# Riding head gates in recurrent weight tiles, compression steps of two chunks, and attention sums in pairs

## The chip, the cores and the metric

One core of a Trainium2 chip. The metric is the device time of one execution in microseconds (us); lower is better. Besides TensorE (PE in the profile, its weight loads PEld) a core has VectorE (DVE), ScalarE (ACT), GpSimd (POOL) and SyncE (SP), whose queue issues the weight transfers here.

## What is computed

Two layers of a first block (mixer of three branches, cross attention, convolutional MLP) and one layer of a second block, on 256 tokens of width 1024, all in float32. The parts that the change touches:

```python
# first block, in each of two layers
out_a = window_attention(aq, ak, av, a_sink)       # 8 heads of 64, 2 key heads
out_b = dense_block_attention(bq, bk, bv)          # the same shape, no mask
...
# second block
(u_rnn, u_gate, q, k_c, v_c, k_s, v_s, k_w, v_w, g_nsa, g_a, g_b) = jnp.split(xn @ w_in, cuts, axis=-1)
h_a = rg_lru(causal_depthwise_conv(u_rnn, conv_w, conv_b), ...)   # u_rnn: 1344 = 12 * 112 columns
...
kc = rmsnorm(compress_blocks(kv(k_c), phi_k_pe, phi_k_w1, phi_k_w2), kc_norm)
vc = compress_blocks(kv(v_c), phi_v_pe, phi_v_w1, phi_v_w2)
gates = jax.nn.sigmoid(g_nsa...)                   # 16 heads x 3 = 48 columns
...
def compress_blocks(z, pe, w1, w2):                # 15 blocks of 32 tokens, 4 groups
    ...
    return jax.nn.gelu(flat @ w1, approximate=True) @ w2
```

## The kernel before

All weights stream through the chip once. `Stream` (L174) brings them in chunks of 128 x 1024 (512 KB): SyncE starts the transfer into `raw` (4 buffers), ScalarE casts it to `wh` (L220), VectorE takes the rest `wl` = `raw` - `wh` (L221), and the product with the activations, themselves split into a high and a low part, is three float32r matmuls for each weight tile (`mm_a`, L402 to L404, or `mm_b`, L416 to L418). A chunk of eight 128-wide tiles is 24 matmuls over the 256 tokens. `take` (L224) gives out a chunk; the next two are split ahead of it.

TensorE's order is written by hand: the order of the calls is its order. Each `take` is followed by a tick (L341), which first gives out what `later(n, f)` has put off by n ticks and then one step of each background generator. So the attention runs between the chunks of other products: `attend` (L721) issues the scores of a unit (two heads, one token tile), `probs_t` (L713) some ticks later, which transposes the probabilities into `pt`, and `sums` some ticks after that. The order of ScalarE and VectorE is made by the tile scheduler, from what the program issues and what waits for what.

`gqa` (L734) makes the units of an attention of block 1. Its `sums` multiply the values with `pt` for two heads at a time: eight matmul records in the trace (four instructions, L757), each with 64 of the array's columns, into one PSUM tile `tp`, which `split` (L386) then takes out: ScalarE the high half `oh` (L388), VectorE the low half `ol` (L389). `tp` (L337) has two buffers; the transposes of `probs_t` use the same name. In each layer there are two attentions of four such sums. `head_norm` (L786) runs beside the first of them; its factor comes from GpSimd (`rstd`, L371), and its second half is L809, the rotation L773, L778 and L784 on VectorE.

In the second block the chunk `gn` holds the 48 columns of the head gates, padded to 128. Its product gives `gs`, which `gates` transposes two ticks later (L1527). Then come the recurrent branch (`lru_steps`, L1244, chunks `ur`, `ug`, `lga`, `lgx`; tiles 112 wide) and, between its first eight chunks, `phi_steps` (L1167), the first layer of the compression MLPs: a `pkv` chunk a step, used in float32 straight from `raw`, eight records with 60 columns each (L1177). `lru_tail` (L1295) and the selected attention `nsa_units` (L1324) run in the background.

```python
ATT = (2,) * 8 + (1, 2) * 4, 4, 2
def tp(self, shape=(128, 4, 128)):
    return self.ps.tile(list(shape), F32, name="tp", bufs=2)
```

Of the kernel before, what the change touches and what calls it, by code (L numbers as in the profile page):

```python
# [19 lines left out]
S = 256  # L20
# [19 lines left out]
TURN = 2  # L40
WARM = 7
# [6 lines left out]
def pack_a(w, nw=128, kw=128, per=8):  # L48
    """[K, N] -> one chunk of `per` stationary tiles after the other, N outer and K inner."""
    k, n = w.shape  # L50
    t = w.reshape(k // kw, kw, n // nw, nw).transpose(2, 0, 1, 3).reshape(-1, kw, nw)
    c = t.shape[0] // per
    return np.ascontiguousarray(t.reshape(c, per, kw, nw).transpose(0, 2, 1, 3).reshape(c, kw, per * nw))


def pack_b(w):
    """[K, N] -> chunks of two 128-row tiles of 512 columns, N outer and K inner."""
    k, n = w.shape
    t = w.reshape(k // 128, 128, n // 512, 512).transpose(2, 0, 1, 3).reshape(-1, 2, 128, 512)
    return np.ascontiguousarray(t.transpose(0, 2, 1, 3).reshape(-1, 128, 1024))  # L60


def feat(v, w=128):
    """[..., N] -> [w, ..., N // w]: features on partitions."""
# [11 lines left out]
def layout(x):  # L76
    """The arrays the program reads: the inputs cut and ordered, and constants of the shapes."""
# [55 lines left out]
def layout2(f, o):  # L133
# [4 lines left out]
    o["ur"], o["ug"] = pack_a(ur, RW), pack_a(ug, RW)  # L138
# [4 lines left out]
    o["gn"] = pack_a(np.pad(gn.reshape(D, 16, 3)[:, :, [1, 2, 0]].transpose(0, 2, 1).reshape(D, 48), ((0, 0), (0, 80))))  # L143
# [30 lines left out]
class Stream:  # L174
    """The weights in the order of their use: each chunk comes in ahead of its products and is split
    into two float32r parts whose sum is the float32 weight."""
# [10 lines left out]
    def load(self, i, piece=None):  # L187
# [7 lines left out]
        else:  # L195
            # the very first chunk, in two pieces of 512 columns
# [46 lines left out]
    def take_last(self, key, places, more):  # L243
        """The last chunks of a product, as many as places and two, and those behind them, all on chip at once;
        those behind the first two have their room in places, the third one behind and on in more."""
# [5 lines left out]
    def hold(self, after):  # L251
        """The next chunks are split after the instructions `after`."""
        self.after, self.until = after, self.split + 2


class Program:
    def __init__(self, ctx, tc, a, out):
# [41 lines left out]
        # products that raise the tensor engine's clock while the first loads are on their way  # L299
# [4 lines left out]
    def order2(self, add):  # L304
        add("q2", len(EARLY))
        for key in ("k2", "v2", "cc", "gn"):
            add(key)
        n = 0
        for kind, b in LRU_ORDER:
            for i in range(2 if kind == "b" else 3):  # L310
                if kind == "b":
                    add("lgx" if i else "lga", b, b + 1)
                else:
                    add("ur" if kind == "u" else "ug", 3 * b + i, 3 * b + i + 1)
                if n < 8:
                    add("pkv", n, n + 1)
                n += 1
        for key in ("ga", "pa", "gb", "pb", "wo2", "minb", "min", "mout"):
            add(key)

    # ---- small helpers
# [18 lines left out]
    # ---- the order of the tensor engine: a tick before the products of each chunk  # L340
    def tick(self):  # L341
        """Gives out what is due, then a step of everything in the background."""
# [14 lines left out]
    def spawn(self, g):  # L357
        """Runs the first step of g now, the others a tick apart."""
# [3 lines left out]
    def wait(self):  # L362
        """What follows on the vector engine comes after the split of the last chunk."""
        return self.tc.issue_after(self.w.last.ins)

    def settle(self):
        """Gives out all that is left in the background."""
# [3 lines left out]
    def rstd(self, pool, var, eps, n, scale=1.0):  # L371
        """(var * scale + eps) ** -0.5 in float32, Newton's method from the exponent halved."""
# [13 lines left out]
    def split(self, h, l, src):  # L386
        """float32r parts h + l of src (SBUF or PSUM)."""
# [7 lines left out]
    def mm_a(self, ps, w, xs, nw=128, kw=128, t0=0, start=True, stop=True):  # L395
        """ps [nw, S] += W^T x: stationary tiles t0.. of the chunk w against the feature-major xs."""
# [9 lines left out]
    def mm_b(self, outs, ws, xs, kt, ts=(0, 1)):  # L406
        """outs[t] [128, 512] += x W for chunk list ws covering k-tiles kt.. of kt_n."""
# [12 lines left out]
    def mm_b_first(self, outs, wt, xs):  # L420
        """mm_b with the very first chunk, in the order in which the parts come."""
# [8 lines left out]
    def proj_b(self, key, xs, kn=8):  # L430
        """Token-major product with a [K, 512] weight."""
# [41 lines left out]
    def turn(self, outs, n, done):  # L473
        """Feature-major tiles [128, 2, S] of a token-major product: done(i, tile) n ticks later."""
# [15 lines left out]
    def take_early(self, key):  # L490
        """Takes the chunks that come before the next one of `key`."""
# [29 lines left out]
    def q(self, op, *args, **kw):  # L521
        """An instruction of the vector engine in the order of these calls."""
# [21 lines left out]
    def to_fm(self, t, halves, dst):  # L544
        """Token tile t, by halves, to its feature-major high parts in dst, then the low parts."""
# [77 lines left out]
        # sums by halves, squares about the mean of the first half: var = E[(x - m0)^2] - (m - m0)^2  # L623
# [59 lines left out]
    def softmax(self, s, scale, sink=None, mask=None):  # L683
        """Scores s (PSUM [128, 2, 256]) of two heads -> normalised probabilities [128, 2, 256]."""
# [28 lines left out]
    def probs_t(self, pr, pt, t):  # L713
        """Probabilities of token tile t transposed into pt [keys, head, key tile, tokens]."""
# [926 lines left out]
```

## Time and profile before

| | |
|---|---|
| time, median of 3 runs | 1471.21 us (1470.07 to 1471.54) |
| profiled execution, its span | 1467.7 us |
| TensorE busy | 1446.2 us, 99% of the span |
| VectorE, ScalarE busy | 1083.6 us, 889.3 us |
| HBM read | 254.89 MB, 174 GB/s |

The runs lie 2.4 to 3.8 us above the span of the profiled execution, which is what the trace covers. A timeline row reads: start in us, duration in us, engine, line, operation, output tile <- input tiles, shape, count, and in brackets the idle time before it and what ended it. The timeline draws consecutive instructions of one kind together, and a matmul's duration is a modelled one that overlaps the next; from start to start is what the engine spends.

### The profile page before, as it was taken

How to read it: one execution, taken by the hardware profiler on the slowest of the kernel's cores; microseconds unless marked ns; L12 is line 12 of the kernel's file. 1: busy time of each engine (PE TensorE's matmuls, PEld its weight loads, DVE VectorE, ACT ScalarE, POOL GpSimd, SP SyncE). 2: the span in 40 equal slices, each digit the busy share in tenths (PEclk: the TensorE clock that was granted, in tenths of full speed). 3: DMA queues.
4: the chain of work that ended last, by engine and by line, in shares of the span. 5: the costliest groups of instructions: out<-in, count | busy, mean ns of one | idle time of the engine just before them, and what ended most of it. 6: DMA issues, size and time to landing. Idle time of an engine off the chain costs nothing.

```text
span 1467.7 us, 26006 instructions
## 1 busy us (share of the span) xinstructions
PE 1446.2 (99%) x9919; PEld 1315.4 (90%) x9919; DVE 1083.6 (74%) x2195; ACT 889.3 (61%) x1608; POOL 46.0 (3%) x134
## 2 busy tenths in 40 slices
PE   9999999999999999999999999999999999999998
PEld 7889988899988899998889998788989999899887
DVE  6887576788857888668688885886889785866543
ACT  5866555666645586555666665464888775555432
POOL 1110000000000020000000000120100000000000
PEclk9999999999999999999999999999999999999999
DMA  8554574555566544454736566356544445555563
GB/s 314 172 159 158 177 225 127 187 188 186 179 186 216 186 145 147 141 197 164 253 105 205 184 199 221 129 171 190 172 121 141 134 149 168 191 164 183 185 202 99
DMA packets 75192, 257.63 MB, mean 176 GB/s; under 512 B 9787, under 2 KB 11196, under 8 KB 74940
## 3 DMA queue, kind: packets, MB, share of 16 engines
q1 hardware_dynamic: 75067, 255.97, 54.5%
q8 instruction: 78, 1.28, 0.3%
q14 instruction: 47, 0.38, 0.1%
HBM read 254.89 MB, written 1.05 MB: 174 GB/s over the span
## 4 chain that ended last, share of the span: by engine, by line
PE 82%; DVE 7%; ACT 5%; DMA 3%; issue 2%; POOL 1%; SPq 0%; DVEq 0%; ACTq 0%; POOLq 0%
PE mm L402 15%; PE mm L403 15%; PE mm L404 15%; PE mm L417 8%; PE mm L418 8%; PE mm L416 8%; DVE wl L221 2%; PE mm L455 2%; PE mm L457 2%; PE mm L458 1%; ACT wh L220 1%; PE tp L718 1%; PE tp L757 1%; PE tp L552 1%; PE sc L680 1%
## 5 line engine op out<-in xcount | busy, mean ns | idle before, releaser
L221 DVE TENSOR_TENSOR wl<-raw,wh 128x1024 fp32r<-128x1024 f32 (+3 forms) x434 | 521.0, 1206 | 236.8 <-ACT wh L220 230.7
L220 ACT CAST wh<-raw 128x1024 fp32r<-128x1024 f32 (+3 forms) x434 | 447.1, 1036 | 403.9 <-PE mm L403 141.3
L402 PE MATMUL mm<-fmh,wh 128*128 128x256 f32 (+1 forms) x1736 | 493.8, 284 | 3.8 <-ACT gates L957 1.7
L403 PE MATMUL mm<-fml,wh 128*128 128x256 f32 (+1 forms) x1736 | 490.6, 283 | 0.0
L404 PE MATMUL mm<-fmh,wl 128*128 128x256 f32 (+1 forms) x1736 | 490.6, 283 | 0.0
L402 PEld LDWEIGHTS mm<-fmh,wh 128*128 128x128 f32 (+1 forms) x1736 | 329.1, 190 | 9.1 <-issue 2.9
L403 PEld LDWEIGHTS mm<-fml,wh 128*128 128x128 f32 (+1 forms) x1736 | 329.2, 190 | 0.2
L404 PEld LDWEIGHTS mm<-fmh,wl 128*128 128x128 f32 (+1 forms) x1736 | 329.4, 190 | 0.0
L416 PE MATMUL mm<-wh,fmh 128*128 128x512 f32 x204 | 81.1, 397 | 0.5 <-ACT wh L220 0.5
L417 PE MATMUL mm<-wl,fmh 128*128 128x512 f32 x204 | 79.8, 391 | 0.8 <-DVE wl L221 0.8
L418 PE MATMUL mm<-wh,fml 128*128 128x512 f32 x204 | 79.9, 392 | 0.0
L416 PE MATMUL mm<-wh,ah 128*128 128x512 f32 x168 | 66.4, 395 | 0.0
L417 PE MATMUL mm<-wl,ah 128*128 128x512 f32 x168 | 66.4, 395 | 0.0
L418 PE MATMUL mm<-wh,al 128*128 128x512 f32 x168 | 66.3, 395 | 0.0
L402 PE MATMUL mm<-oh,wh 128*128 128x256 f32 x192 | 54.4, 283 | 0.0
L404 PE MATMUL mm<-oh,wl 128*128 128x256 f32 x192 | 53.8, 280 | 0.0
L403 PE MATMUL mm<-ol,wh 128*128 128x256 f32 x192 | 53.8, 280 | 0.0
L417 PE MATMUL mm<-wl,zh 128*128 128x512 f32 x128 | 50.6, 395 | 0.0
L418 PE MATMUL mm<-wh,zl 128*128 128x512 f32 x128 | 50.6, 395 | 0.0
L416 PE MATMUL mm<-wh,zh 128*128 128x512 f32 x128 | 50.6, 395 | 0.0
L1057 ACT ACTIVATE k<-mm,featp 128x256 f32<-128x256 f32 x88 | 48.6, 559 | 0.0
L417 PEld LDWEIGHTS mm<-wl,fmh 128*128 128x128 f32 x204 | 38.4, 188 | 8.7 <-DVE wl L221 1.1
(391 smaller groups left out, 2635.4 us busy)
## 6 DMA issues: line engine op xcount, KB each, us to landing
raw<-in_up_dram SPq DMA_DIRECT2D x80, 512.0 KB, 3.5
raw<-in_gate_dram SPq DMA_DIRECT2D x48, 512.0 KB, 3.5
raw<-in_down_dram SPq DMA_DIRECT2D x44, 512.0 KB, 3.5
raw<-in_mout_dram SPq DMA_DIRECT2D x32, 512.0 KB, 4.3
raw<-in_min_dram SPq DMA_DIRECT2D x28, 512.0 KB, 3.6
raw<-in_br_dram SPq DMA_DIRECT2D x24, 512.0 KB, 3.5
raw<-in_mix_dram SPq DMA_DIRECT2D x16, 512.0 KB, 3.5
raw<-in_wo_dram SPq DMA_DIRECT2D x16, 512.0 KB, 3.5
```

The lines of the kernel that those rows point to most:

```text
L220: self.nc.scalar.copy(h[:p, :w], r[:p, :w])
L221: self.last = self.nc.vector.tensor_sub(l[:p, :w], r[:p, :w], h[:p, :w].bitcast(F32))
L402: self.nc.tensor.matmul(ps, wh[:kw, c], xh[k], start=start and k == 0, stop=False)
L403: self.nc.tensor.matmul(ps, wh[:kw, c], xl[k], start=False, stop=False)
L404: self.nc.tensor.matmul(ps, wl[:kw, c], xh[k], start=False, stop=stop and k == n - 1)
L416: self.nc.tensor.matmul(outs[t], xh[:, k, r], wh[:, c], start=k == 0, stop=False)
L417: self.nc.tensor.matmul(outs[t], xh[:, k, r], wl[:, c], start=False, stop=False)
L418: self.nc.tensor.matmul(outs[t], xl[:, k, r], wh[:, c], start=False, stop=k == k_all - 1)
L455: self.nc.tensor.matmul(outs[t], xl[:, k, r], wh, start=False, stop=k == 7)
L457: self.nc.tensor.matmul(outs[t], xh[:, k, r], wh, start=k == 0, stop=False)
L458: self.nc.tensor.matmul(outs[t], xh[:, k, r], wl, start=False, stop=False)
L1057: nc.scalar.activation(y[:, i], ps, AF.Identity, bias=cb[:, c:c + 1], scale=k[1])
```

## The change

Three edits. (1) The chunk `gn` goes; its 48 columns are dealt to the first three tiles of `ur`, 16 each, which become 128 wide in a key of their own, `ur0`; ScalarE copies each 16 (as part of rows 96 to 127) into a third of `gs`, and `gates` is issued two ticks after the third of these chunks, with transposes of 96 rows. (2) `phi_steps` takes two `pkv` chunks at a step, at the steps 3, 5, 7 and 9 of `lru_steps` in place of 1 to 8. (3) `sums` takes a list: in the windowed attention two and two, in the other two, one and one. The two PSUM tiles of a pair are allocated first, then the matmuls of both, then both splits.

```diff
+PHI = 3, 5, 7, 9
...
-    o["ur"], o["ug"] = pack_a(ur, RW), pack_a(ug, RW)
+    gn = gn.reshape(D, 16, 3)[:, :, [1, 2, 0]].transpose(0, 2, 1)
+    first = np.concatenate([ur[:, :3 * RW].reshape(D, 3, RW), gn], 2).reshape(D, 384)
+    o["ur0"], o["ur"], o["ug"] = pack_a(first), pack_a(ur[:, 3 * RW:], RW), pack_a(ug, RW)
...
-            def sums(p, g, at):
-                op = self.tp((128, S))
-                for k in range(2):
-                    for j in range(2):
-                        nc.tensor.matmul(op[j * 64:j * 64 + 64], v[:, k, g * 64:g * 64 + 64], at["pt"][:, j, k],
-                                         start=k == 0, stop=k == 1)
-                self.split(o[0][:, p], o[1][:, p], op)
-                whole.append(p)
+            def sums(held):
+                ops = [self.tp((128, S)) for _ in held]
+                for op, (p, g, at) in zip(ops, held):
+                    for k in range(2):
+                        for j in range(2):
+                            nc.tensor.matmul(op[j * 64:j * 64 + 64], v[:, k, g * 64:g * 64 + 64], at["pt"][:, j, k],
+                                             start=k == 0, stop=k == 1)
+                for op, (p, g, at) in zip(ops, held):
+                    self.split(o[0][:, p], o[1][:, p], op)
+                    whole.append(p)
...
-        units = (self.gqa(q[0], kz[0], va, rowp[:, :8], self.wmask, o[0], ready[0], self.whole[0]),
-                 self.gqa(q[1], kz[1], vb, None, None, o[1], ready[1], self.whole[1]))
+        units = (self.gqa(q[0], kz[0], va, rowp[:, :8], self.wmask, o[0], ready[0], self.whole[0], (2, 2)),
+                 self.gqa(q[1], kz[1], vb, None, None, o[1], ready[1], self.whole[1], (2, 1, 1)))
...
-        for c in range(8):
-            raw = self.w.take("pkv").rearrange("p (i q n) -> p i q n", i=2, n=256)
-            for q in range(2):
+        for c in range(0, 8, 2):
+            raws = [self.w.take("pkv").rearrange("p (i q n) -> p i q n", i=2, n=256) for _ in range(2)]
+            for q in range(4):
...
-                    self.mm_a(ps[:RW], w.take("ur"), self.fmk(xs), nw=RW)
+                    if b:
+                        self.mm_a(ps[:RW], w.take("ur"), self.fmk(xs), nw=RW)
+                    else:
+                        self.mm_a(ps, w.take("ur0"), self.fmk(xs))
+                        nc.scalar.copy(gs[32 * i:32 * i + 32], ps[96:])
```

What this makes of the order, at two places. TensorE, the windowed attention of layer 0, the second sums of the trace (89.78); L757 is the sums, L718 the transposes of the next probabilities, L680 and L681 the scores behind them. Before:

```order
L402 MATMUL mm<-fmh,wh 128x256
L403 MATMUL mm<-fml,wh 128x256
L404 MATMUL mm<-fmh,wl 128x256
L757 MATMUL tp<-k_743,v 64x256 x4
L718 MATMUL tp<-ident,pr 128x128 x4
L680 MATMUL sc<-k_158,q_154 128x256
L681 MATMUL sc<-k_159,q_154 128x256
L680 MATMUL sc<-k_158,q_155 128x256
```

and now (the lines are five to seven further down):

```order
L407 MATMUL mm<-fmh,wh 128x256
L408 MATMUL mm<-fml,wh 128x256
L409 MATMUL mm<-fmh,wl 128x256
L764 MATMUL tp<-k_575,v 64x256 x4
L764 MATMUL tp<-k_743,v 64x256 x4
L723 MATMUL tp<-ident,pr 128x128 x4
L685 MATMUL sc<-k_158,q_154 128x256
L686 MATMUL sc<-k_159,q_154 128x256
```

The sums of the unit before (`k_575`) have moved down to here, and `tp` is written three times in a row.

VectorE at the same place; `ol` is the low half of a sum, L784 (now L797) the end of the head norm, L691 (L696) the masked scores that TensorE makes behind the transposes. Before:

```order
L710 TENSOR_SCALAR pr<-pr,sm_s 128x256 x2
L784 TENSOR_TENSOR k_1107<-k_1108,k_1109 128x512
L691 ISA pr,sm_m<-sc,wmask 128x256
L691 ISA sm_m 128x1
L691 ISA pr,sm_m<-sc,wmask 128x256
L691 ISA sm_m 128x1
L389 TENSOR_TENSOR ol<-tp,oh 128x256
```

and now:

```order
L715 TENSOR_SCALAR pr<-pr,sm_s 128x256 x2
L797 TENSOR_TENSOR k_1100<-k_1101,k_1102 128x512
L394 TENSOR_TENSOR ol<-tp,oh 128x256 x2
L224 TENSOR_TENSOR wl<-raw,wh 128x1024
L696 ISA pr,sm_m<-sc,wmask 128x256
L696 ISA sm_m 128x1
```

Both `ol` now stand together behind the head norm and ahead of the masked scores. At the first pair of the other attention, VectorE, before:

```order
L695 TENSOR_REDUCE sm_m<-sc 128x2
L221 TENSOR_TENSOR wl<-raw,wh 128x1024
L700 TENSOR_SCALAR sm_n<-sm_m 128x2
L221 TENSOR_TENSOR wl<-raw,wh 128x1024
L695 TENSOR_REDUCE sm_m<-sc 128x2
L708 RECIPROCAL sm_s<-sm_s 128x2
L389 TENSOR_TENSOR ol<-tp,oh 128x256
```

and now:

```order
L700 TENSOR_REDUCE sm_m<-sc 128x2
L224 TENSOR_TENSOR wl<-raw,wh 128x1024
L705 TENSOR_SCALAR sm_n<-sm_m 128x2
L224 TENSOR_TENSOR wl<-raw,wh 128x1024
L394 TENSOR_TENSOR ol<-tp,oh 128x256 x2
L700 TENSOR_REDUCE sm_m<-sc 128x2
L713 RECIPROCAL sm_s<-sm_s 128x2
```

The two `ol` stand behind the same weight split, and ahead of the next scores' maxima.

## Rows read from the trace of the kernel before

**Rows 1.** The page: engines' busy time; shares of the chain that ended last

```profile
PE 1446.2 (99%) x9919; PEld 1315.4 (90%) x9919; DVE 1083.6 (74%) x2195; ACT 889.3 (61%) x1608; POOL 46.0 (3%) x134
...
PE 82%; DVE 7%; ACT 5%; DMA 3%; issue 2%; POOL 1%; SPq 0%; DVEq 0%; ACTq 0%; POOLq 0%
```

**Rows 2.** Timeline of TensorE around sums (L757); a late window starts inside a group

```profile
75.12 0.28 PE L404 MATMUL mm<-fmh,wl 128*128 128x256 f32 x1
75.33 1.08 PE L757 MATMUL tp<-k,v 128*64 128x256 f32 x8
76.35 0.65 PE L718 MATMUL tp<-ident,pr 128*128 128x128 f32 x4
...
75.60 0.82 PE L757 MATMUL tp<-k,v 128*64 128x256 f32 x6
...
89.78 1.08 PE L757 MATMUL tp<-k,v 128*64 128x256 f32 x8
...
147.82 1.08 PE L757 MATMUL tp<-k,v 128*64 128x256 f32 x8
...
556.18 1.08 PE L757 MATMUL tp<-k,v 128*64 128x256 f32 x8
```

**Rows 3.** Timeline of VectorE, layer 0, windowed attention

```profile
78.81 0.42 DVE L389 TENSOR_TENSOR ol<-tp,oh 128x256 fp32r<-128x256 f32 x1
...
93.53 0.69 DVE L784 TENSOR_TENSOR k<-k,k 128x512 f32<-128x512 f32 x1
```

**Rows 4.** Stretch: its length, then busy time of PE, PEld, DVE, ACT, POOL; clock, DMA

```profile
84.17:94.55 10.38, 10.38 (x88) 9.72 (x87) 10.38 (x30) 5.18 (x13) 0.00 (x0) 1.00 0.43 129
```

**Rows 5.** Timeline of VectorE, layer 1, windowed attention

```profile
550.38 0.69 DVE L809 TENSOR_TENSOR k<-mm,rs_y 128x512 f32<-128x512 f32 x1
...
557.96 0.61 DVE L710 TENSOR_SCALAR pr<-pr,sm_s 128x256 f32<-128x256 f32 x2
...
559.49 0.69 DVE L784 TENSOR_TENSOR k<-k,k 128x512 f32<-128x512 f32 x1
```

**Rows 6.** Timeline of VectorE, layer 0, the other attention

```profile
148.94 1.23 DVE L221 TENSOR_TENSOR wl<-raw,wh 128x1024 fp32r<-128x1024 f32 x1 [1.97 <-ACT wh L220]
...
150.75 0.40 DVE L389 TENSOR_TENSOR ol<-tp,oh 128x256 fp32r<-128x256 f32 x1
```

**Rows 7.** Timeline of TensorE: gate transposes (L1527) and the first compression step (L1177)

```profile
1001.85 0.32 PE L1527 MATMUL tp<-ident,k 48*128 48x48 f32 x2
1002.10 1.08 PE L1177 MATMUL sc<-raw,k 128*60 128x256 f32 x8
1003.11 0.37 PE L402 MATMUL mm<-fmh,wh 128*112 128x256 f32 x1
1003.32 0.28 PE L403 MATMUL mm<-fml,wh 128*112 128x256 f32 x1
```

**Rows 8.** Stretches: four of whole chunks or VectorE's load, two of the clock

```profile
996.07:998.95 2.88, 2.88 (x27) 2.88 (x25) 2.79 (x5) 1.31 (x2) 0.00 (x0) 1.00 0.10 11
1034.79:1037.61 2.82, 2.82 (x27) 2.82 (x26) 1.00 (x2) 2.76 (x6) 0.00 (x0) 1.00 0.94 302
1084.78:1089.64 4.86, 4.86 (x24) 4.86 (x25) 3.62 (x12) 3.23 (x7) 0.00 (x0) 0.55 0.71 251
1065.00:1075.00 10.00, 10.00 (x87) 10.00 (x86) 9.92 (x18) 8.32 (x13) 0.00 (x0) 1.00 0.32 94
107.00:108.00 1.00, 0.00 (x0) 0.00 (x0) 0.92 (x4) 0.96 (x3) 0.00 (x0) 1.00 0.00 0
1082.00:1083.00 1.00, 1.00 (x8) 1.00 (x8) 1.00 (x2) 1.00 (x7) 0.00 (x0) 0.65 0.90 258
```

**Rows 9.** Timeline of TensorE: three matmuls that waited

```profile
108.38 0.39 PE L402 MATMUL mm<-fmh,wh 128*128 128x256 f32 x1 [1.66 <-ACT gates L957]
...
1053.21 0.24 PE L1220 MATMUL tp<-ident,k 60*128 60x60 f32 x1 [1.07 <-DVE k L1216]
...
1079.92 0.34 PE L402 MATMUL mm<-xch,wh 112*112 112x256 f32 x1 [0.86 <-DVE nm L1373]
```

More of the change, by code (lines that the diff above doesn't have):

```diff
@@ L142, in layout2 @@
     o["cc"] = pack_a(np.concatenate([kc, vc], 1))
-    o["gn"] = pack_a(np.pad(gn.reshape(D, 16, 3)[:, :, [1, 2, 0]].transpose(0, 2, 1).reshape(D, 48), ((0, 0), (0, 80))))
     o["ga"], o["gb"] = pack_a(ga), pack_a(gb)
@@ L305, in order2 @@
         add("q2", len(EARLY))
-        for key in ("k2", "v2", "cc", "gn"):
+        for key in ("k2", "v2", "cc"):
             add(key)
@@ L312, in order2 @@
                     add("lgx" if i else "lga", b, b + 1)
-                else:
-                    add("ur" if kind == "u" else "ug", 3 * b + i, 3 * b + i + 1)
-                if n < 8:
-                    add("pkv", n, n + 1)
+                elif kind == "u":
+                    add("ur" if b else "ur0", 3 * max(b - 1, 0) + i, 3 * max(b - 1, 0) + i + 1)
+                else:
+                    add("ug", 3 * b + i, 3 * b + i + 1)
                 n += 1
+                if n in PHI:
+                    add("pkv", 2 * PHI.index(n), 2 * PHI.index(n) + 2)
         for key in ("ga", "pa", "gb", "pb", "wo2", "minb", "min", "mout"):
@@ L732, in attend, with gqa @@
                 yield
-    def gqa(self, qt, kz, v, sink, mask, o, ready, whole):
+    def gqa(self, qt, kz, v, sink, mask, o, ready, whole, together):
         nc = self.nc
+        held, together = [], list(together)
         while not ready:
@@ L751, in scores @@
                                      None if mask is None else mask[:, t])
-            def sums(p, g, at):
-                op = self.tp((128, S))
-                for k in range(2):
-                    for j in range(2):
-                        nc.tensor.matmul(op[j * 64:j * 64 + 64], v[:, k, g * 64:g * 64 + 64], at["pt"][:, j, k],
-                                         start=k == 0, stop=k == 1)
-                self.split(o[0][:, p], o[1][:, p], op)
-                whole.append(p)
+            def sums(held):
[8 more added lines that the diff above has]
+                    whole.append(p)
+            held.append((p, g, at))
+            last = None
+            if len(held) == together[0]:
+                last = partial(sums, held)
+                held, together = [], together[1:]
             for t in range(2):
                 yield (partial(scores, p, g, t, at), lambda t=t, at=at: self.probs_t(at[t], at["pt"], t),
-                       partial(sums, p, g, at) if t else None)
+                       last if t else None)
     def rope_mul(self, out, x, tab, nh, w, pool, dup=False):
@@ L1171, in phi_steps @@
         hp = self.sc((128, 256))
-        for c in range(8):
-            raw = self.w.take("pkv").rearrange("p (i q n) -> p i q n", i=2, n=256)
-            for q in range(2):
+        for c in range(0, 8, 2):
+            raws = [self.w.take("pkv").rearrange("p (i q n) -> p i q n", i=2, n=256) for _ in range(2)]
+            for q in range(4):
                 pp = 2 * c + q
                 for i in range(2):
-                    nc.tensor.matmul(hp[64 * i:64 * i + 60], zts[i][:, pp], raw[:, i, q],
+                    nc.tensor.matmul(hp[64 * i:64 * i + 60], zts[i][:, pp], raws[q // 2][:, i, q % 2],
                                      start=pp == 0, stop=pp == 15)
@@ L1242, in lru_rate, with lru_steps @@
         nc.vector.tensor_scalar(rp[:, 5 * RT:7 * RT], rp[:, 5 * RT:7 * RT], 0.5, None, op0=OP.mult)
-    def lru_steps(self, xs, ya, pool, prm):
+    def lru_steps(self, xs, ya, pool, prm, gs, gates):
         nc, w = self.nc, self.w
@@ L1263, in lru_steps @@
                     yield
+                if not b:
+                    self.later(2, gates)
                 xh = pool.tile([RW, 3, S], F32R, name="xch", bufs=1)
@@ L1518, in block2 @@
                 zts.append(zt)
-            ps = self.mm((128, S))
-            self.mm_a(ps, w.take("gn"), self.fmk(xs))
-            gs = self.k2((48, S))
-            nc.scalar.copy(gs, ps[:48])
+            gs = self.k2((96, S))
             def gates():
                 for t in range(2):
-                    tp = self.tp((128, 48))
-                    nc.tensor.transpose(tp, gs[:, t * 128:t * 128 + 128], self.ident[:48, :48])
-                    gv = gt[:, t].rearrange("p b h -> p (b h)")
-                    nc.scalar.activation(gv, tp, AF.Tanh, scale=0.5)
+                    tp = self.tp((128, 3, 32))
+                    nc.tensor.transpose(tp.rearrange("p b h -> p (b h)"), gs[:, t * 128:t * 128 + 128],
+                                        self.ident[:96, :96])
+                    gv = gt[:, t]
+                    nc.scalar.activation(gv, tp[:, :, 16:], AF.Tanh, scale=0.5)
                     nc.vector.tensor_scalar(gv, gv, 0.5, 0.5, op0=OP.mult, op1=OP.add)
                 nc.vector.tensor_scalar(gt[:, 0, 2], gt[:, 0, 2], cval, None, op0=OP.mult)
-            self.later(2, gates)
             ya, self.yp = [], pool
@@ L1542, in block2 @@
                 prm = rp[:, :4 * RT], rp[:, 4 * RT:5 * RT], rp[:, 5 * RT:6 * RT], rp[:, 6 * RT:7 * RT], cl
-                for i, _ in enumerate(self.lru_steps(xs, ya, lp, prm)):
-                    if i < 8:
+                for i, _ in enumerate(self.lru_steps(xs, ya, lp, prm, gs, gates), 1):
+                    if i in PHI:
                         next(phi)
-                    elif i == 8:
+                    if i == PHI[-1]:
                         self.back.append(phi)
```

## The prediction

> **What bounds the kernel now.** The page comes first. TensorE is busy for 1446.2 of 1467.7 us and 82% of the chain that ended last is its own work [rows 1]. So a matmul taken away is worth what it held TensorE for, and a wait put in front of TensorE is worth its whole length. Next, TensorE's timeline around the sums of block 1 [rows 2]: the reader is to see that the transposes of the next probabilities (L718) follow the sums (L757) at once, with no wait. Then VectorE's timeline at the same places [rows 3, 5, 6], which says when the low half `ol` of such a sum is taken out of PSUM, and the stretches table [rows 4], which says whether VectorE has a gap there. Last, the recurrence and compression stage [rows 7 to 9].
>
> The sum is made against the profiled execution, whose span is 1467.7 us. The median of the runs is 1471.21 us, 3.5 us more, and I add the same difference to the forecast. I take 0.2%, 2.9 us, as what can be told from no change.
>
> **What is saved.**
> Gate chunk: 24 matmuls in 2.88 us go. Three chunks of `ur` become 128 wide; a 128-wide chunk takes 2.88 us and a 112-wide one 2.82 us [rows 8], so 3 x 0.06 = 0.18 us comes back. The two gate transposes take 0.25 us (1001.85 to 1002.10) [rows 7]; they now stand alone between chunks, not ahead of a compression step, and I add 0.15 us for a switch of their own. Net 2.55 us. The DMA, the cast and the split of that chunk go too; they lay beside TensorE's work and are counted at nothing, as are the three small copies by ScalarE that replace one.
> How a wider tile loads is a place where rule and row differ: the Trainium skill ("TensorE: Matmul & The Clock Gate", LDWEIGHTS) lets a load grow with its columns, P / 1.2 ns, which for 16 more columns in 72 tiles would be an estimated 0.96 us. The chunks here differ by 0.18 us in all [rows 8], so the trace does not show that price.
>
> Sums in pairs: from the last ordinary matmul before a group (75.12) to the transposes behind it (76.35) is 1.23 us where the next matmul would have come after 0.12 (2.88 us for 24 [rows 8]), so a group costs 1.11 us. Of its eight records the last six start at 75.60, and between there and 76.35 lie three pairs, of which the last also pays the switch out (0.32 us); a pair inside costs (0.75 - 0.32) / 2 = 0.22 us [rows 2]. Four more matmul pairs inside another group cost 0.86 us. One merge gives 0.25 us; three a layer and two layers make 1.5 us.
> Compression in pairs: the groups have the same form (1002.10 to 1003.11) and the matmul behind one takes 0.21 us where 0.12 is usual [rows 7], so a merge gives 0.25 + 0.09 = 0.34 us, and four give 1.35 us.
> Together **5.4 us saved**.
>
> **What is added: a wait of the transposes.** There are two `tp` tiles in PSUM. The sums used one and the transposes behind them the other. Now a pair of sums takes both, so the transposes behind them wait until VectorE has taken `ol` from the first. The order shows where that `ol` stands.
> First pair, layer 0: VectorE has no gap from 84.17 to 94.55 [rows 4], and `ol` now stands behind the last step of the head norm (L784, 93.53 to 94.22) [rows 3]. Before, this sum's `ol` ran at 78.81, long ahead of it. TensorE reaches the pair 1.11 us earlier, at 88.67 instead of 89.78 [rows 2], and wants the transposes 1.02 + 0.86 us later, at 90.55. `ol` starts as L784 ends, at 94.2, and takes 0.42 us [rows 3]: the tile is free at 94.6. Stall 4.05 us.
> First pair, layer 1: wanted at 556.18 - 1.11 + 1.88 = 556.95 [rows 2]. The second half of that norm starts at 550.38, when GpSimd has its factor, and L784 ends at 560.18 [rows 5]. Two scalings join this stretch (0.61 us) and one score pass, about half as long, leaves it; with `ol` behind it the tile is free near 560.7. Stall 3.75 us.
> Last pair of each layer: `ol` stands behind the split of a weight chunk, which starts at 148.94 (1.97 us of waiting for its cast) and ends at 150.17 [rows 6]. The pair starts at 147.82 [rows 2] and is over at 149.70; `ol` ends at 150.5. Stall 0.85 us, twice, since layer 1 has the same rows shifted.
> The middle pairs are followed by scores and a whole chunk, not by transposes; their `ol` is cheap to reach, and I count nothing.
> Together **9.5 us added**. Behind the waiting transposes stand the next scores and all later chunks, so the whole chain moves.
> The Trainium skill ("Perfetto Trace Analysis", Optimizing Tensor Performance) asks that independent groups rotate through different PSUM banks, so that evacuation overlaps the next group; it speaks against taking both tiles at once. Going by it alone, with no rows, one would only know the sign.
>
> **What comes back of it, and what follows.**
> Layer 0 waits at 108.38 for `gates` (1.66 us) [rows 9]. A TensorE that is late would not wait there. But the program also moves ScalarE's and VectorE's work at this place: the next masked scores now stand behind a memory split, so `gates` comes later too. Between 0 and 1.66 us come back; I take 0.
> Clock: the granted clock fell to its lower level (0.5, 1.2 GHz) in this trace only after several waits close together, at 1082 [rows 8], behind waits of which the first ended at 1079.92 [rows 9]; a single hole of 1.9 us kept 1.00 (108.38 [rows 9]; 107 to 108 shows no TensorE work at all [rows 8]). Two stalls of about 4 us are twice as long as any single hole here. A chunk at the lower level takes 4.86 us for 2.88 [rows 8], so a fall costs about 2.0 us. In layer 0 I expect it to be swallowed by the wait for `gates`; in layer 1 nothing swallows it: **2.0 us added**, between 0 and 3.2 (from 1082.65 to 1089, 6.4 us at half speed, if a fall lasts as long as this one; the chunk at 1084.78 ends it [rows 8]).
> Recurrence stage: VectorE is nearly full there (9.92 of 10 us from 1065 to 1075) [rows 8]. The wait at 1053.21 for a normalised key (1.07) [rows 9] shrinks, since the norm of the compressed keys follows closer on their last step: at most 1.07 us back, I take 0.9. But one weight split and one product over three tiles, which ran ahead of the first selected softmax, now stand behind it on VectorE, which TensorE then waits for at 1079.92 [rows 9]: about a microsecond each (a split of a whole chunk takes 1.23 [rows 6]), 2.1 us lost. Net **1.2 us added**, between -1 and +4.
>
> **The sum.** -5.4 + 9.5 + 0 + 2.0 + 1.2 = +7.3 us: a span of 1475.0, and 1478.5 us as the time. Slower by 0.5%.
>
> **The rivals.**
> A. *The stall does not come* (faster). It decides at one point: whether `ol` of the first pair ends before 90.5. For it: TensorE's savings are sure. Against: VectorE would have to be 4 us ahead in a stretch without a gap [rows 4], which begins with a wait for GpSimd that the change does not touch. Time: 1471.2 - 5.4 + 1.2 = 1467.0 us.
> B. *The stall comes and is mostly given back*: the clock stays at full speed, the 1.66 us at 108.38 come back, and the recurrence stage loses nothing. -5.4 + 9.5 - 1.7 = +2.4: 1473.6 us, not to be told from no change. For it: no single hole in the trace lowered the clock [rows 8].
> C. *The clock falls in both layers and stays low for longer*, and the recurrence stage loses its 4 us: -5.4 + 9.5 + 2 x 3.2 + 2.8 = +13.3: 1484.5 us. For it: the waits from 1079 on already pull the clock down [rows 8].
> D. *The change moves less than it says.* The program has fewer matmuls by exactly one chunk and the groups are merged as written, so this has little chance; it would leave 1471 us.
>
> **Chances and range.** Forecast 0.5, A 0.1, B 0.2, C 0.15, D 0.05. The range takes in the forecast, B down to 1471 and C up to its end: 1470.5 to 1484.5. Faster by over 0.2%: A and a little of B, 0.11. Within 0.2%: most of B, D and the low edge of the forecast, 0.2. Slower: 0.69.
>
> **What would show each step.** The group of L757 (new L764) should be 16 records at the merged places, about 1.9 us long, and the transposes behind the first pairs should start about 4 us later with VectorE's `ol` as their releaser; behind the last pairs 0.85 us. The compression groups should be 16 records in four places. The granted clock should fall near 95 and 561. If TensorE starts those transposes without a wait, the forecast is wrong and A is right; if it waits 4 us there and the time is still 1471, something gives it back, and the wait at `gates` is where to look.

## The result, and the profile after

The changed kernel takes **1482.05 us** (median of 4 runs, 1481.54 to 1484.71) against 1470.64 for the kernel before (1468.05 to 1471.54): 1.0082 times as long, 95% interval 1.0068 to 1.0097, or 11 to 12 us more. The forecast was 1478.5 us in 1470.5 to 1484.5. The profiled execution of the changed kernel took 1484.71 us, 2.7 us over its median, with a span of 1482.9.

The page after, busy times and the chain (compare [rows 1]):

```profile
PE 1449.1 (98%) x9895; PEld 1320.4 (89%) x9895; DVE 1085.1 (73%) x2194; ACT 889.3 (60%) x1609; POOL 45.7 (3%) x134
...
PE 83%; DVE 6%; ACT 5%; DMA 4%; issue 1%; POOL 0%; SPq 0%; DVEq 0%; ACTq 0%
```

24 matmul records have gone and TensorE is busy for 2.9 us more. So a part of its work got slower, which is a matter of the clock. The table of waits on TensorE says where it stood still (engine, line, what it waited for: us in all, times, longest):

```profile
PE tp L723 <- DVE ol L394: 8.9, 4, 3.9
PE mm L407 <- ACT lga L1309: 2.0, 1, 2.0
...
PE mm L407 <- DVE xc L1277: 1.0, 1, 1.0
PE mm L407 <- ACT wh L223: 1.0, 1, 1.0
PE tp L1201 <- issue: 0.8, 1, 0.8
...
PE sc L1190 <- DMA raw<-in_pkv_dram: 0.7, 1, 0.7
```

The first row is the forecast's wait: four times, 8.9 us. There is no row for `gates`, for which the kernel before waited 1.66 us [rows 9]. TensorE's timeline at the first pair of layer 0, the last pair of layer 0 and the first pair of layer 1:

```profile
89.70 1.95 PE L764 MATMUL tp<-k,v 128*64 128x256 f32 x16
95.51 1.11 PE L723 MATMUL tp<-ident,pr 128*128 128x128 f32 x4 [3.86 <-DVE ol L394]
...
151.68 1.95 PE L764 MATMUL tp<-k,v 128*64 128x256 f32 x16
154.41 0.66 PE L723 MATMUL tp<-ident,pr 128*128 128x128 f32 x4 [0.78 <-DVE ol L394]
...
561.78 1.95 PE L764 MATMUL tp<-k,v 128*64 128x256 f32 x16
567.21 0.66 PE L723 MATMUL tp<-ident,pr 128*128 128x128 f32 x4 [3.48 <-DVE ol L394]
```

and VectorE's at the same places:

```profile
94.43 0.69 DVE L797 TENSOR_TENSOR k<-k,k 128x512 f32<-128x512 f32 x1
95.03 0.75 DVE L394 TENSOR_TENSOR ol<-tp,oh 128x256 fp32r<-128x256 f32 x2
...
152.79 1.22 DVE L224 TENSOR_TENSOR wl<-raw,wh 128x1024 fp32r<-128x1024 f32 x1 [1.97 <-ACT wh L223]
153.94 0.75 DVE L394 TENSOR_TENSOR ol<-tp,oh 128x256 fp32r<-128x256 f32 x2
...
566.14 0.68 DVE L797 TENSOR_TENSOR k<-k,k 128x512 f32<-128x512 f32 x1
566.74 0.74 DVE L394 TENSOR_TENSOR ol<-tp,oh 128x256 fp32r<-128x256 f32 x2
```

Two sums are now 16 records in one row. The transposes start as the first of two `ol` ends; that `ol` stands behind the end of the head norm (L797) at the first pairs and behind a weight split at the last. Of the clock the stretches say (length; busy PE, PEld, DVE, ACT, POOL; granted clock, DMA share, GB/s):

```profile
94.00:95.00 1.00, 0.00 (x0) 0.00 (x0) 1.00 (x3) 0.45 (x2) 0.00 (x0) 0.62 0.74 270
95.00:100.00 5.00, 4.49 (x21) 4.50 (x22) 3.46 (x10) 1.59 (x3) 0.00 (x0) 0.50 0.85 256
100.00:102.00 2.00, 2.00 (x15) 2.00 (x14) 1.54 (x4) 1.78 (x6) 0.00 (x0) 0.73 0.67 246
...
568.00:572.00 4.00, 4.00 (x23) 4.00 (x23) 1.96 (x9) 1.68 (x6) 0.00 (x0) 0.59 0.38 132
```

Behind both long waits the clock is at its lower level, 1.2 GHz. Last, the compression steps (L1190) and what follows them:

```profile
1044.65 1.08 PE L1190 MATMUL sc<-raw,k 128*60 128x256 f32 x8
1046.46 1.08 PE L1190 MATMUL sc<-raw,k 128*60 128x256 f32 x8 [0.73 <-DMA raw<-in_pkv_dram]
1048.50 0.37 PE L407 MATMUL mm<-fmh,wh 128*112 128x256 f32 x1 [0.96 <-ACT wh L223]
...
1052.28 0.41 PE L407 MATMUL mm<-fmh,wh 128*112 128x256 f32 x1
...
1054.82 0.41 PE L1201 MATMUL tp<-ident,k 128*128 128x128 f32 x2 [0.82 <-issue]
```

The last pair waits between its two chunks, the chunk behind it for a cast (0.96; ScalarE had stood idle for 3.82 us until that chunk's transfer came) and then for a split (0.64), its matmuls take 0.41 us for 0.28 (the lower clock again), and the transposes of the hidden layer (L1201) start as ScalarE ends their Gelu, at 1054.7:

```profile
1052.66 1.28 ACT L1197 ACT_TABLE_LOAD   x1
1053.95 0.77 ACT L1197 ACTIVATE k<-sc 60x256 f32<-60x256 f32 x2
```

How far the changed kernel is behind, by the starts of the same matmuls in the two profiled executions, less the 1.37 us that its start-up took longer (first transposes of probabilities at 59.98 before, 61.34 after):

| place | before | after | behind |
|---|---|---|---|
| 11th transposes of probabilities, layer 0 | 137.31 | 141.23 | 2.55 |
| last of layer 0 | 262.92 | 268.50 | 4.21 |
| last of layer 1 | 723.51 | 735.68 | 10.80 |
| key norm of the second block | 984.17 | 999.40 | 13.87 |
| last product of `lga`, `lgx` | 1119.27 | 1134.78 | 14.14 |

The 3.1 us between 723 and 984 are this execution's: in the profile of the first experiment, with the same sums, that stretch costs 0.4. The granted clock was down there twice, 0.50 from 736 to 739 and from 948 to 950, behind waits of 1.91 and 1.80 us; the first experiment has waits of 1.61 and 1.86 us at the same two places, and its clock stayed up. The later start is a fall of the clock too (0.50 from 13 to 15). Edit 2 alone, with the sums of before, has the same one: it starts 0.88 us later, waits 0.35 us for `gates` in place of 1.66 and ends layer 0 at 262.20. There the wait takes the late start up, which the changed kernel can't; counted without that correction, its layer 0 is 5.6 us behind.

### The profile page after: what moved, and what is told of

The parts are those of the page before. It is cut to its first block, busy times and chain, and to the rows that moved or that the text cites. A ratio compares the mean times of both kernels' runs of the same rounds, so it can differ in the third digit from the quotient of the medians.

```text
span 1482.9 us, 25957 instructions
## 1 busy us (share of the span) xinstructions
PE 1449.1 (98%) x9895; PEld 1320.4 (89%) x9895; DVE 1085.1 (73%) x2194; ACT 889.3 (60%) x1609; POOL 45.7 (3%) x134
## 3 DMA queue, kind: packets, MB, share of 16 engines
q8 instruction: 78, 1.28, 0.3%
## 4 chain that ended last, share of the span: by engine, by line
PE 83%; DVE 6%; ACT 5%; DMA 4%; issue 1%; POOL 0%; SPq 0%; DVEq 0%; ACTq 0%
PE mm L407 16%; PE mm L408 16%; PE mm L409 16%; PE mm L422 8%; PE mm L423 8%; PE mm L421 8%; DVE wl L224 2%; PE mm L462 2%; PE mm L460 2%; PE mm L463 2%; ACT wh L223 2%; PE tp L723 1%; DMA raw<-in_kv_dram 1%; PE tp L557 1%; PE sc L685 1%
## 5 line engine op out<-in xcount | busy, mean ns | idle before, releaser
L421 PEld LDWEIGHTS mm<-wh,fmh 128*128 128x128 f32 x204 | 38.7, 190 | 9.3 <-ACT wh L223 1.6
```

Source lines behind the costliest of these rows:

```text
L421: self.nc.tensor.matmul(outs[t], xh[:, k, r], wh[:, c], start=k == 0, stop=False)
```

## The experiments

The theory on record: the waits for `ol` are the loss, the clock adds to it, and the other two edits save less than they should. The first four runs take the change apart.

**One edit at a time.**

```diff
 e1_sums_only:   edit 3 stays, edits 1 and 2 are undone
 e2_gates_only:  edit 1 stays, edits 2 and 3 are undone
 e3_steps_only:  edit 2 stays, edits 1 and 3 are undone
```

> Only edit (3): sums in pairs, the gate chunk and the compression steps as before. Theory W (the pair takes both tp tiles, the transposes behind it wait for VectorE's ol, and the clock falls after the two long waits): the same waits of about 4.2, 0.85 + 0.3, 3.9 and 0.85 + 0.3 us as in the changed kernel, the granted clock at 0.50 for some microseconds behind the two long ones, nothing in the recurrence stage; 1479 to 1483 us, so nearly the whole loss of the change. Rival R (the loss comes from the recurrence stage and from edits 1 and 2): at most 1473 us.

Measured: 1481.54 us, 1.0076 (1.0059 to 1.0092). The sums alone are nearly the whole loss, with the same 8.9 us of waits.

> Only edit (1): the gate columns ride in three ur tiles; sums one by one, compression a chunk a step. The sum of the prediction: 2.5 us less than before, 1467.5 to 1468.8 us. Rival: the wider tiles cost a weight load of 13 ns more in 72 places and the three copies delay the convolution on ScalarE, so that no more than 1 us is left: 1469.5 to 1471 us.

Measured: 1469.49 us, 0.9995 (0.9982 to 1.0008): 0.7 us less, but the interval goes from 2.6 us less to 1.2 more, so the time alone can't tell the forecast 2.55 us from nothing. One place that takes some back is the first compression step. The gate chunk stood ahead of it and gave VectorE time; without it the step waits in its midst:

```profile
998.79 0.64 PE L1190 MATMUL sc<-raw,k 128*60 128x256 f32 x2
1000.16 1.04 PE L1190 MATMUL sc<-raw,k 128*60 128x256 f32 x6 [0.72 <-DVE k L1536]
```

> Only edit (2): two pkv chunks a step. Theory N (two pkv chunks hold two of the four raw buffers until TensorE has read them, so the transfers behind them start late): TensorE waits for a transfer or a cast around the last two steps, 2 to 4 us in all, and the time is 1470 to 1473 us, not faster. Rival (four merged groups, nothing else): 1.35 us less, 1469.2 us, and no wait for a pkv transfer.

Measured: 1473.45 us, 1.0026 (1.0015 to 1.0037): slower by 3.8 us where the merges should have given 1.35. TensorE doesn't wait for a transfer, as expected, but for ScalarE: the transposes of the hidden layer (L1200) start 2.40 us late. A late transfer stands behind it, though: ScalarE's cast at 1033.27 had waited 2.71 us for its chunk, where the one at 1031.82 in the kernel before waited 0.28. Whether that is the cause is tested below.

**Both sums of a pair in one PSUM tile.** All three edits, but a pair of sums takes two halves of one `tp` tile, so the transposes behind it have the other tile.

```diff
-                ops = [self.tp((128, S)) for _ in held]
+                op = self.tp((128, n, S))
...
-                for op, (p, g, at) in zip(ops, held):
-                    self.split(o[0][:, p], o[1][:, p], op)
+                self.split(o[0][:, p:p + n], o[1][:, p:p + n], op)
```

> The changed kernel, but a pair of sums goes into the two halves of one tp tile (512 columns) and is split by one cast and one subtraction, so the second tp tile stays free for the transposes. Theory W: the four waits for ol are gone and the clock stays at full speed there; edits 1 and 2 are still in, with the recurrence stage as in the changed kernel; 1468.5 to 1471 us, 11 to 13 us below the changed kernel. Rival (the transposes would have waited anyway, for VectorE's probabilities behind the same head norm): the wait moves to pr, and the time stays above 1477 us.

Measured: 1472.95 us, 1.0013 (1.0000 to 1.0025), above the 1468.5 to 1471 that were expected. No wait for `ol` is left, and 9.1 us of the loss have gone with it: the second tile is what TensorE waited for. But a wait for `gates` stands in layer 0 again, and it is longer than the 1.66 us of before:

```profile
107.62 0.39 PE L407 MATMUL mm<-fmh,wh 128*128 128x256 f32 x1 [2.81 <-ACT gates L971]
```

**The clock.** Edit 3 alone, with TensorE kept busy during the first pairs' waits: 16 matmuls of the identity with itself, whose result nobody reads.

```diff
+                if len(held) == 2 and mask is not None and not whole:
+                    fill = self.sc((128, 128))
+                    for _ in range(16):
+                        nc.tensor.matmul(fill, self.ident, self.ident, start=True, stop=True)
```

> Edit 3 alone, with sixteen matmuls of the identity with itself (their result is not used) between the first pair of sums and the transposes of the windowed attention in each layer: they lie in the time in which TensorE would otherwise stand still for `ol`, about 4 us. Edit 3 alone took 1481.5 us, ratio 1.0076. Theory: a part of that loss is the clock, which falls behind the two long waits; with TensorE busy through them the granted clock stays 1.00 at 94 to 102 and at 568 to 574, and the time falls by about 3 us, to 1478.5 (ratio 1.0055, between 1.0045 and 1.0065). Rival: the clock's fall lies beside other waits and costs nothing by itself: 1481.5, ratio 1.0076 within 0.0007, though the clock stays up.

Measured: 1476.45 us, 1.0041 (1.0026 to 1.0056), against 1.0076 (1.0059 to 1.0092) without the filling: about 5 us less, with more matmuls. (The two intervals leave 2 to 8 us; 3 were expected.) TensorE still waits as long for `ol`; it only isn't idle:

```profile
88.33 1.95 PE L763 MATMUL tp<-k,v 128*64 128x256 f32 x16
90.21 3.84 PE L768 MATMUL sc<-ident 128*128 128x128 f32 x32
94.16 0.66 PE L722 MATMUL tp<-ident,pr 128*128 128x128 f32 x4
...
109.77 0.38 PE L406 MATMUL mm<-fmh,wh 128*128 128x256 f32 x1 [0.84 <-ACT gates L973]
```

The stretches behind the first pair, without the filling:

```profile
95.00:100.00 5.00, 5.00 (x24) 5.00 (x25) 3.77 (x12) 2.56 (x5) 0.00 (x0) 0.50 0.82 293
100.00:102.00 2.00, 2.00 (x15) 2.00 (x15) 0.97 (x3) 1.46 (x6) 0.00 (x0) 0.74 0.42 124
```

and with it:

```profile
95.00:100.00 5.00, 5.00 (x45) 5.00 (x44) 3.37 (x10) 2.25 (x4) 0.00 (x0) 1.00 0.84 263
```

In the 5 us from 95 TensorE gets through 24 records at the lower level and 45 at the higher. With the filling the wait for `gates` is back (0.84), so in layer 0 a part of what the clock costs did lie beside that wait.

**The one-tile sums by themselves, and with the gate edit.**

```diff
 e8_one_alone:       the sums as in e4_one_tile; edits 1 and 2 undone
 e5_gates_one_tile:  the same, with edit 1
```

> Only the sums are changed, and a pair of them is written into two halves of one PSUM tile. Theory: six merges of 0.25 us are the gain, 1.5 us: 1468.7 us, ratio 0.999. Rival: layer 0's part (0.75 us) goes into a longer wait for `gates` at about 107, which ends when ScalarE is done and not when TensorE comes: 1469.4 us, ratio 0.9995.

> Edit 1, and the pairs of sums in two halves of one PSUM tile; the compression takes a chunk a step, as before. Theory: the two gains add and no wait for `ol` appears. Edit 1 alone read -0.7 us; the one-tile pairs should be worth their six merges of 0.25 us: together 1468 us, ratio 0.9985. Rival: the time that TensorE gains in layer 0 is eaten by the wait for `gates` (2.8 us there with one-tile pairs in the changed kernel, 1.66 in the kernel before), so about half of the merges' gain goes: 1469 us, ratio 0.999. If edit 1 were worth the 2.55 us that were forecast for it, the time would be 1466.2 us.

Measured: 1471.84 us, 1.0006 (0.9992 to 1.0020) for the sums alone, and 1469.53, 0.9993 (0.9980 to 1.0006) with the gate edit. The two part by 1.9 us, which is not clear of noise, and the merges show nothing at all in the time. Where they stand they do what was forecast: a pair holds TensorE for 1.97 us (89.71 to 91.80, less the usual 0.12) where two groups took 2 x 1.11, so a merge saves the 0.25 us. The timeline in layer 0 says where that goes:

```profile
89.71 0.28 PE L408 MATMUL mm<-fmh,wl 128*128 128x256 f32 x1
89.92 1.95 PE L764 MATMUL tp<-k,v 128*64 128x256 f32 x16
91.80 0.66 PE L722 MATMUL tp<-ident,pr 128*128 128x128 f32 x4
...
109.09 0.58 PE L406 MATMUL mm<-fmh,wh 128*128 128x256 f32 x1 [2.52 <-ACT gates L970]
```

```profile
107.00:109.00 2.00, 0.00 (x0) 0.00 (x0) 1.90 (x6) 1.96 (x7) 0.00 (x0) 1.00 0.77 256
109.00:110.00 1.00, 0.91 (x4) 0.92 (x5) 0.95 (x2) 1.00 (x3) 0.00 (x0) 0.56 0.61 213
110.00:114.00 4.00, 4.00 (x26) 4.00 (x26) 3.20 (x4) 1.92 (x4) 0.00 (x0) 0.68 0.36 136
```

The wait for `gates` is 2.52 us where it was 1.66, and behind it the clock falls, which it did not behind the 1.66. The rival of this run had only the longer wait; the clock on top of it makes the edit worth nothing. From the matmul that waited for `gates` to the next transposes of probabilities it is 6.32 us in the kernel before (108.38 to 114.70) and 7.82 here (109.09 to 116.91).

**Why the pairs of compression steps lose.** First the place: a step earlier.

```diff
-PHI = 3, 5, 7, 9
+PHI = 2, 4, 6, 8
```

> Edit 2 alone, with the pairs of chunks at the steps 2, 4, 6 and 8 in place of 3, 5, 7 and 9. Edit 2 alone took 1473.5 us, ratio 1.0026, with a wait of 2.4 us at the transposes of the hidden layer. Theory L: the loss is the lead: the last pair comes a step later than the last single chunk did, so the hidden layer is wanted right behind its sum. A step earlier that wait is gone and 2.4 us come back: 1471.0 us, ratio 1.0005 or less. Theory R: the loss is the raw buffers, two of whose four a pair of chunks holds, so that transfers behind it start late and ScalarE and VectorE fall behind; the step's number changes nothing in that: 1473.5 us, ratio 1.0026, with waits of about the same sum at other places.

Measured: 1478.33 us, 1.0051 (1.0039 to 1.0064). Slower still, and the wait of the hidden layer stays (1.87 us); new ones stand behind it, 1.78 and 0.89 us for `ks` and 2.72 for `ug`. This did not test the lead, though: what follows the last pair begins when its step is done (`i == PHI[-1]`), so it moved up with it. Then the raw buffers: the chunks of the compression are left out of the stream.

```diff
-            raws = [self.w.take("pkv")... for _ in range(2)]
+            for _ in range(2):
+                self.tick()
+            raws = [self.stale] * 2
```

> The kernel before, with the eight chunks of the compression's first layer left out of the stream: the steps multiply with what lies in a resident tile of the same shape, so no transfer and no raw buffer belongs to them. All matmuls and ticks stay; the compressed keys are not those of the reference. It is the base for the next run. Since the transfers are beside TensorE's work for the most part, 1468 to 1470 us, ratio 0.9985 to 1.0000.

> Edit 2 alone (two chunks a step, at the steps 3, 5, 7 and 9), again with the compression's chunks left out of the stream and a resident tile in their place. Theory R: what edit 2 lost (3.8 us against the kernel before, where a gain of 1.35 us was forecast) comes of the pair of chunks in the raw buffers; without them the pairs are faster than the single steps of the run beside this one by the four merges, 1.35 us (0.09%). Rival O: the loss comes of where the steps and their followers stand in ScalarE's and VectorE's order; then the pairs stay slower than the single steps, by 3 to 4 us (0.2 to 0.27%).

Measured: 1470.15 us, 1.0004 (0.9992 to 1.0016) for the single steps and 1473.25, 1.0023 (1.0010 to 1.0036) for the pairs. With no transfer and no buffer the pairs lose as before, about 2.8 us against the run beside them, where theory R had them 1.35 us faster. So R falls as the cause, and it goes as rival O has it; the intervals are too wide to say that late transfers add nothing to the 3.8 us of edit 2 alone. The output of both runs is computed with the wrong weights, as said. The wait is still there:

```profile
1041.02 0.66 PE L1200 MATMUL tp<-ident,k 128*128 128x128 f32 x2 [2.87 <-ACT k L1196]
```

What it waits for is a Gelu on ScalarE. Its timeline with edit 2 alone:

```profile
1036.26 1.28 ACT L1324 ACT_TABLE_LOAD   x1
1037.56 0.85 ACT L1324 ACTIVATE lga<-lga 112x768 f32<-112x768 f32 x1
1038.42 1.28 ACT L1196 ACT_TABLE_LOAD   x1
1039.71 0.77 ACT L1196 ACTIVATE k<-sc 60x256 f32<-60x256 f32 x2
```

and in the kernel before (L1184 is the Gelu, L1312 the other function):

```profile
1033.15 1.28 ACT L1184 ACT_TABLE_LOAD   x1
1034.45 0.38 ACT L1184 ACTIVATE k<-sc 60x256 f32<-60x256 f32 x1
1034.73 0.59 ACT L1307 ACTIVATE lga<-lga,cl 112x256 f32<-112x256 f32 x1
1035.33 0.38 ACT L1184 ACTIVATE k<-sc 60x256 f32<-60x256 f32 x1
...
1038.02 1.28 ACT L1312 ACT_TABLE_LOAD   x1
```

Before, the last compression step ended at 1031.87 and the transposes came at 1037.61, two chunks later: 5.7 us in which ScalarE loaded a table (1.28) and was done by 1035.7. With the last pair at step 9 one chunk lies between (the pair ends at 1034.26, the transposes could start at 1038.2), and ScalarE takes up the other function first, with a table load of its own. So the steps go a step earlier and what follows them begins where it did:

```diff
-PHI = 3, 5, 7, 9
+PHI = 2, 4, 6, 8
...
-                    if i == PHI[-1]:
+                    if i == PHI[-1] + 1:
```

> Edit 2 alone, with its pairs at the steps 2, 4, 6 and 8, and what follows them still begun at step 9, as in the kernel before. Theory L, put right: in the kernel before a whole chunk lies between the last compression step and the step that issues the Gelu, and the transposes of the hidden layer come a chunk behind that; with the last pair at step 9 (or at 8 with the followers begun at 8) this lead is 2.9 us shorter, while ScalarE needs 1.28 us for each change of its function table besides the Gelu itself, so the transposes wait 2.4 to 3.1 us. With the lead of the kernel before, that wait is gone and the four merges are left: 1470.2 - 1.35 = 1468.9 us, ratio 0.9991. Rival: other waits of the stage make most of the loss; then the ratio stays at 1.002 to 1.003 (1473 to 1475 us) though no wait stands ahead of those transposes.

Measured: 1471.00 us, 1.0008 (0.9997 to 1.0020), against 1.0026 for the pairs at 3, 5, 7 and 9. The run of the pairs a step earlier differs from this one only in where the followers begin, and it took 1.0051: 6.3 us, with the intervals well apart. The transposes start without a wait; ScalarE is through with the Gelu at 1037.84:

```profile
1037.98 0.41 PE L1200 MATMUL tp<-ident,k 128*128 128x128 f32 x2
```

Against edit 2 alone about 2.6 us come back by the ratios (1.3 by the medians; the intervals overlap), and the merges' 1.35 still don't show; what takes those is not settled. This profile has a wait of 1.13 us for the normalised key (0.52 in the kernel before), 0.64 for a split at 1032 (none there before) and 1.6 for `lga` (1.01).

**All three edits, mended.**

```diff
 e13_best:  edit 1; edit 2 as in e12_steps_lead; edit 3 as in e4_one_tile
```

> All three edits mended: the head gates in the recurrent tiles, the compression's pairs at 2, 4, 6 and 8 with the lead of the kernel before, and the pairs of sums in two halves of one PSUM tile. The gate edit read -0.7 and -1.9 us in two comparisons, the pairs of steps should give 1.35, the one-tile sums gave nothing by themselves (the wait for `gates` at 105 took it): 1467.5 us, ratio 0.998. Rival: layer 0's wait for `gates` and the recurrence stage, where VectorE and ScalarE set the pace, take what TensorE gains: 1470 us, ratio 1.000.

Measured: 1468.67 us, 0.9998 (0.9987 to 1.0009). Not to be told from the kernel before: the rival. Its waits for `gates` (2.8 us) and `lga` (1.6 us) are there.

**One stage in all these profiles.** The medians scatter by more than the savings, but the stage that edits 1 and 2 change can be read by itself, from the key norm of the second block to the last product of `lga` and `lgx` (starts of the same matmuls; the kernels with edit 1 have a chunk less in it):

| run | key norm | last product | between |
|---|---|---|---|
| kernel before | 984.17 | 1119.27 | 135.10 |
| sums in pairs alone | 996.51 | 1131.30 | 134.79 |
| sums in pairs, filled | 990.90 | 1124.77 | 133.87 |
| one-tile sums alone | 987.88 | 1122.64 | 134.76 |
| edit 1 alone | 983.78 | 1114.95 | 131.17 |
| edit 1 and one-tile sums | 986.97 | 1119.12 | 132.15 |
| edit 2 alone | 984.71 | 1120.60 | 135.89 |
| edit 2 with the lead | 983.82 | 1119.31 | 135.49 |
| all three, as changed | 999.40 | 1134.78 | 135.38 |
| all three, mended | 987.04 | 1119.16 | 132.12 |

In the first four the stage's program is the same, and it takes 133.9 to 135.1 us. With edit 1 and the single steps it takes 131.2 and 132.2, by the means 3.0 us less (the profile of edit 1 alone is of the fastest of its runs). That is not the chunk alone: TensorE's waits there grow, and the clock, which falls at 1082 in the kernel before [rows 8] and reads 0.50 from 1086 to 1091 with the one-tile sums alone, stays at 1.00 from 1070 to 1100 in both runs with edit 1. All three edits mended bring this stage to 132.12 too, and lose the gain in layer 0, which ends at 265.73 where it ended at 262.92. The mended edits 1 and 2 with the sums one by one were not run.

## Why the prediction held, and where it was off

- **The waits for `ol`**: forecast 4.05, 3.75 and twice 0.85 us, 9.5 in all, behind L784 and behind a split. Measured 3.86, 3.48 and 0.78, 8.9 in all over the four, behind those very instructions. Right; rival A (that VectorE is early enough) is out, and the run with one tile shows that the second tile was the cause. The rule cited ahead, from the Trainium skill ("Perfetto Trace Analysis", Optimizing Tensor Performance), that independent groups should rotate through different banks, is borne out in part: the transposes had no free tile to go to, and 9.1 us hung on that, but what mended it was to put two groups of sums into one tile, not to spread them.
- **Layer 0, gates and clock**: forecast that nothing is left of both, since the clock's fall goes into the wait for `gates`. The wait is gone and the layer ends 4.21 us behind; the forecast's terms there are 4.05 + 0.85 - 0.75 = 4.15. Right in the sum; singly, two misses cancel. With the clock kept up by the filling, 0.84 of the 1.66 us are still waited, so the stalls alone give 0.8 back where 0 was forecast; the clock costs 1.1 us or more there (next point) where 0 was forecast.
- **The clock in all**: forecast 2.0 us (0 and 2.0). The filling took about 5 us off the medians; in the two profiles the runs of the sums and of the filling part by 1.1 us in layer 0 (2.4 if the later start isn't taken off) and by 2.7 in layer 1; the rest lies where nothing was filled. It fell in both layers, as rival C had it. Mis-sized by 1.8 to 3 us: the step took one chunk at half speed for the price; from 95 on, 5 us ran at 0.50 and 2 more at 0.73.
- **What is saved**: forecast 5.4 us. The sizes were right on TensorE itself: a merge of sums gives 0.25 us, and with edit 1 alone its stage is some 3 us shorter in the profiles, waits and clock included, for the 2.55 that were forecast. What failed is that the savings would reach the end. Of the sums' 1.5 us nothing is found in the time (a longer wait for `gates`, and the clock behind it), of the compression's 1.35 nothing either. "A matmul taken away is worth what it held TensorE for" is true only where nothing behind it waits for another engine.
- **The recurrence stage**: forecast +1.2 us, for a split and a product behind the softmax. The wait for the normalised key (1.07) is gone, as forecast, but the wait for `nm` did not grow (0.86 before, 0.8 after), so the reason for the loss was wrong. Edit 2 lost 3.8 us by itself where its merges and this reason together came to about -0.2, and the part of it that was found is the shortened lead of the Gelu (a wait of 2.40 us), which the prediction did not look at. This is the step that failed most. In the changed kernel the stage with both edits should have become 2.55 + 1.35 - 1.2 = 2.7 us shorter; it became 0.3 longer, with new waits for a transfer (0.73), a cast (0.96), a split (0.64), the Gelu (0.82) and `xc` (1.01), and 2.02 for `lga` where there were 1.01.
- **The sum**: +7.3 us forecast, +11.4 measured by the medians. By places, in the profiles, layer 0 is as forecast (or 1.4 us worse, by how the later start is counted), layer 1 is 6.6 us for 5.85, and the stage of the recurrence and compression is 3.0 us worse, which is most of the 4 us between. Two slips in the working change little: rival C names a loss of 4 us and adds 2.8 (with 4 it would end at 1485.7), and the fall of the clock that is said to begin at 1082.65 began at 1082.30 by its own row (0.65 over that microsecond is 0.50 for 0.7 of it).

## What to carry to other kernels

Before two PSUM tiles are taken at once, look at what is transposed or summed next into the same name, and at where the instruction that frees the first stands in its engine's order: merging six groups was to save 1.5 us and cost 8.9 us of waits and a lower clock behind them. A step that is moved takes its followers along or leaves them: count the chunks between a product and the first matmul that needs it, with the table loads of ScalarE in between. And a saving in front of a fixed wait is not a saving: it lengthens the wait, and a longer wait can cost the clock as well.

## What the runs showed of the hardware

- The clock fell to 1.2 GHz at each of the two waits of 3.86 and 3.48 us, and not at the one of 1.66 [rows 9]. Between, the length of the wait does not settle it: with the one-tile sums alone it fell behind 2.52 us, and with the pairs a step earlier it stayed at 1.00 (1092 to 1096) behind 2.72; at the hidden layer's transposes it stayed at 1.00 (1040 to 1044) behind 2.40 us with edit 2 alone. Behind the wait of 3.86 us 95 to 100 ran at 0.50 and 100 to 102 at 0.73.
- Matmuls of no use, in time in which TensorE would stand still, kept the clock at 1.00 and saved about 5 us by the medians, 3.8 to 5.1 by the places.
- ScalarE's change of function is a row of its own, 1.28 us, and it is paid again when two functions alternate: twice between 1036.26 and 1039.71 with edit 2 alone. The Trainium skill ("ScalarE: Activation LUTs", What ACT_TABLE_LOAD costs) counts 1283 ns for the load, as these rows do, and a drain of about 1.38 us on top; the rows leave no place for that: the function before ends at 1038.41, the load starts at 1038.42, and the Gelu starts at 1039.71.
